# The up product's low parts of the two leading columns, multiplied in one run with the high columns

## Chip, cores and metric

The kernel runs on one core of a Trainium2 chip. The metric is device time in microseconds (us): the median of several runs, compared between the kernel before and the kernel after. TensorE multiplies matrices and adds into PSUM banks; VectorE (DVE) and ScalarE (ACT) do everything else on tiles in SBUF, GpSimd (POOL) does next to nothing here, and SyncE (SP) issues nearly all DMAs, in order.

## The reference

One layer of a decoder trunk, in float32, over 1024 tokens behind 16 meta tokens, with width 1024. Two mixers (a convolution branch and a sliding-window attention) are merged by gates; behind them stands a convolutional feed-forward part, which is where the change lies:

```python
    h = layer_norm(DEEPNORM_ALPHA * h + mixed @ w_out, ln1_g, ln1_b)
    up = causal_dwconv(h @ ffn_w_up, ffn_dw, ffn_dw_b)
    u, g = jnp.split(up, 2, axis=-1)
    f = (jax.nn.gelu(g, approximate=False) * u) @ ffn_w_down
    return layer_norm(DEEPNORM_ALPHA * h + f, ln2_g, ln2_b)
```

`ffn_w_up` is 1024 x 5632, `ffn_w_down` 2816 x 1024. The convolution has three taps over tokens and is causal, so each output token needs the up product of its own token and of the two before it.

## The kernel before

**Two-part numbers.** TensorE multiplies rounded float32 numbers. Each operand is split into a high part (ScalarE copies it into the rounded type) and a low part (VectorE subtracts the high part from the number). A product is then three matmuls: high weights with high tokens, high weights with low tokens, low weights with high tokens, all added into one bank.

**The up product.** `h @ ffn_w_up` is done in 22 chunks (`c`), each of 128 columns of u and the 128 columns of g that belong to them. A chunk is a Strassen-like product of two-by-two blocks, with seven products in place of eight. The token operand's seven blocks are B11, B21, BT2, BT1, BT3, BT4 and B22, sums and differences of quadrants (half of the model width, half of the tokens); the weights' seven are made chunk by chunk by `up_weights` (sums on L1426, splits in `wsplit`, L1408 and L1409). Each product has four steps of k (128 rows each), and each step the three matmuls above, on L1599.

**Token blocks.** The 512 tokens of each half are cut in two blocks, `SUB`, of 258 and 256 columns. The two columns more are the two leading columns that the convolution needs: block 0 starts two tokens early. B11, B21, BT2 and BT4 carry them (258 columns in block 0); BT1, BT3 and B22 don't (256), as `columns` says. For the second half the leading columns are those at the end of the first half, and L1652 copies them over.

**Banks.** Four PSUM tiles of 1024 columns hold the sums: pw (V4), px (X), pz (Z), py (Y). Block 0 lies in columns 254 to 511 of one bank and block 1 in 512 to 767 of the next. ScalarE copies X and Y out (L1611), VectorE forms the four results (L1607): c11 and c21 (with the leading columns), c12 and c22. `conv_ffn` applies the three taps: one ScalarE pass (L1523), two VectorE multiply-adds (L1524, L1525). After the gelu (L1529) and the product with the gate (L1533), the result is stored to DRAM (`fd`).

**Where the operands come from.** The low and high parts of the tokens are made once, by `bsplit` (L1279, L1284), from sums formed on L1288. Block 1's are ready first, so chunk 0 runs in two passes: block 1 alone, then block 0, for which the last rows of tokens are turned, summed and split while TensorE multiplies block 1. From chunk 1 on each product runs block 0 and block 1 one after the other (24 matmuls). The weights are split nine products ahead (`w_ahead`).

**Order.** On each engine the order of instructions is fixed when the program is built: a scheduler simulates the engines and takes, of the instructions that are ready, the one of lowest rank (`rank`; 400 for the evacuations of the up product, 470 for the tokens' sums, 500 for weight splits), with a few orders written by hand (`after`, `line`). So a new instruction may move others.

**Behind it.** The down product starts as soon as the last chunk's banks allow. Its operands are read back from `fd`, from `w_down`, or from sums of them (`sd`, `td`, formed on L1553 to L1563), cast on L1702, split on L1703 and multiplied on L1745. Its first product takes six pairs of operands; the sixth holds the last chunk's result.

The places of the tokens' blocks and the matmul loop:

```python
        return t[:, o + hl * 4 * n:o + (hl + 1) * 4 * n]
...
                        for j, (x, hl) in enumerate(((ah, 0), (ah, 1), (al, 0))):
                            ins = nc.tensor.matmul(o, x[:, ks], bmat(sub, q, hl, k), start=first and k + j == 0,
                                                   stop=k == 3 and j == 2, skip_group_check=not first)
```

Of the kernel before, what the change touches and what calls it, by code (L numbers as in the profile page):

```python
# [25 lines left out]
AF = mybir.ActivationFunctionType  # L26
# [75 lines left out]
def tile_hybrid_layer(  # L102
# [1136 lines left out]
    def columns(sub, q):  # L1239

        a, b = SUB[sub]
        return (2 if q in (BT1, BT3, B22) else a) if sub == 0 else a, b

    def bsum(sub, q, hl):
        a, b = columns(sub, q)
        n = b - a
        t, o = B_AT[sub][q]
        return t[:, o + hl * 4 * n:o + (hl + 1) * 4 * n]

    def bmat(sub, q, hl, k):  # L1250
        a, b = columns(sub, q)
        n = b - a
        return bsum(sub, q, hl)[:, k * n:(k + 1) * n]

    lined, high = [], []

# [9 lines left out]
    def wide(x):  # L1266
        return x.rearrange("p (k n) -> p k n", k=4)
# [4 lines left out]
    def bsplit(sub, q, src, cs=slice(None)):  # L1272
        with rank(RK_SUMS):
            a = columns(sub, q)[0] - SUB[sub][0]
            x, y, _ = cs.indices(SUB[sub][1] - SUB[sub][0])
            x = max(x, a)
            hi, lo = (wide(bsum(sub, q, hl))[:, :, x - a:y - a] for hl in range(2))
            src = wide(src)[:, :, x:y]
            ins = nc.scalar.copy(hi, src)  # L1279
            if (sub, q) in ((0, BT2), (0, BT4), (0, BT1), (0, BT3)):  # L1280
                if high:
                    after(ins, high[-1])
                high.append(ins)
            line(nc.vector.tensor_tensor(lo, src, f32(hi), OP.subtract))  # L1284

    def bsub(out, x, y, cs=slice(None)):
        with rank(RK_SUMS):
# [227 lines left out]
        ft_next[0] += 1  # L1515
        return FA[:, i * 512:(i + 1) * 512]

    c11, c21, u2 = (FA[:, 4128 + i * HW:4128 + (i + 1) * HW] for i in range(3))
    c12, c22, u13 = (RT[:, i * HW:(i + 1) * HW] for i in range(3))

    def conv_ffn(cc, o):
        t = ftmp()
        nc.scalar.activation(t, cc[:, 2:HW], AF.Identity, bias=ffw(3, o), scale=ffw(2, o))  # L1523
        nc.vector.scalar_tensor_tensor(t, cc[:, 1:HW - 1], ffw(1, o), t, OP.mult, OP.add)  # L1524
        nc.vector.scalar_tensor_tensor(t, cc[:, 0:HW - 2], ffw(0, o), t, OP.mult, OP.add)  # L1525
        return t

    def gelu(t):
# [40 lines left out]
    for c in range(FC):  # L1569
        if c == 1:  # L1570
            wo_stack.close()
            sums_p = ctx.enter_context(tc.tile_pool(name="sums", bufs=1, side="right", reuse_waits="tile"))
            RXF, SM1 = (sums_p.tile([P, 2048], F, name=n) for n in ("raw", "sums"))
            for i in range(FC):
                SM[i] = [(OB[:, 2048:4096], SM1)[i % 2][:, h * 1024:(h + 1) * 1024] for h in range(2)]
        V4, X, Z, Y = (pup.tile([P, 1024], F, name=n, tag=n) for n in ("pw", "px", "pz", "py"))
        passes = ((1,), (0,)) if c == 0 else ((0, 1),)
        for subs in passes:
            last = subs == passes[-1]
            w_next = iter(range(7))  # L1580
            a, b = SUB[subs[0]][0], SUB[subs[-1]][1]
            i = max(a, 2)

            def at(t, a=a):
                return t[:, 254 + a:254 + b]

            def prod(q, bank, first):
                if last:
                    w_ahead(9)
                    ah, al = w_ready.pop(0)  # L1590
                else:
                    ah, al = w_ready[next(w_next)]
                for sub in subs:
                    x, y = columns(sub, q)
                    o = bank[:, 254 + x:254 + y]
                    for k in range(4):
                        ks = slice(k * P, (k + 1) * P)
                        for j, (x, hl) in enumerate(((ah, 0), (ah, 1), (al, 0))):
                            ins = nc.tensor.matmul(o, x[:, ks], bmat(sub, q, hl, k), start=first and k + j == 0,  # L1599
                                                   stop=k == 3 and j == 2, skip_group_check=not first)  # L1600
                            if k + j == 0 and last_mm:
                                after(ins, last_mm[-1])
                    last_mm.append(ins)

            def tt(*x):
                with rank(RK_CHAIN):
                    return nc.vector.tensor_tensor(*x)  # L1607

            def copy(*x):
                with rank(RK_CHAIN):  # L1610
                    copied.append(nc.scalar.copy(*x))  # L1611
# [36 lines left out]
            if last:  # L1648
                with rank(RK_CHAIN):
                    ends, starts = (t.rearrange("p (i n) -> p i n", i=2)[:, :, x:x + 2]  # L1650
                                    for t, x in ((FA[:, 4128:4128 + 2 * HW], HW - 2), (RT[:, 0:2 * HW], 0)))
                    nc.vector.tensor_copy(starts, ends)  # L1652
# [278 lines left out]
```

## Time and profile before

| | |
|---|---|
| median of 3 runs | 1236.19 us (1235.96 to 1236.53) |
| span of the profiled execution, first to last instruction | 1234.6 us |
| TensorE's mean granted clock in it | 0.999 |
| up product (first to last start of a matmul of L1599) | 589.4 to 1017.3 us |
| of it chunk 0, in two passes | 589.4 to 611.2 us |
| down product | 1017.3 to the end |

The profile is of one execution; its own time is given as the span alone, and what lies around the span is the distance to the median. PE stands for TensorE's matmuls, PEld for its weight loads. A row of the timeline gives the start in us from the span's first instruction, the time from the start of the first to the end of the last instruction that it merges, then engine, line, operation, the tiles written and read, the shape, and the count; in brackets the idle time before it and what ended that. The ends of matmuls overlap with the next ones, so the pace of TensorE is read from the distance of starts.

### The profile page before, as it was taken

To read this page: it belongs to the slowest core of one execution; us is meant where nothing else is said; L and a number is where in the kernel's file an instruction comes from. 1 tells how busy PE (TensorE), PEld (TensorE's weight loads), DVE (VectorE), ACT (ScalarE), POOL (GpSimd) and SP (SyncE) were. 2 spreads that over 40 slices of the span, in tenths; PEclk is the share of its full clock that TensorE was granted. 3 is DMA by queue.
4 is the path that set the end of the run, shared out by engine and by line. 5 is a ranking of instruction groups with operands and counts; after the bars stand their busy time and mean duration, and the time that the engine had idled before them with its cause. 6 is when DMAs were issued, how large, how long until landed. Compare 5 with 4: busy or idle time off the path is not lost.

```text
span 1234.6 us, 21810 instructions
## 1 busy us (share of the span) xinstructions
PE 1225.2 (99%) x8568; PEld 1141.5 (92%) x8568; DVE 1085.2 (88%) x1842; ACT 584.7 (47%) x1065; POOL 15.6 (1%) x20
## 2 busy tenths in 40 slices
PE   9999999999999999999999999999999999999997
PEld 8999989999999999888999999999999998888886
DVE  8899989999879798659899999998999986996697
ACT  7532336654255223345755545555455554445331
POOL 1000000000000010000000000000000000000000
PEclk9999999999999999999999999999999999999999
DMA  7396834412255655322255555554455568988722
GB/s 282 74 298 151 210 98 116 127 55 73 82 158 163 183 140 144 104 85 87 66 171 207 191 187 205 188 183 142 172 203 190 178 239 304 391 315 312 256 86 85
DMA packets 109152, 213.02 MB, mean 173 GB/s; under 512 B 31883, under 2 KB 46779, under 8 KB 108922
## 3 DMA queue, kind: packets, MB, share of 16 engines
q1 hardware_dynamic: 93050, 200.56, 49.5%
q10 hardware_dynamic: 16000, 11.07, 2.9%
q8 instruction: 67, 1.10, 0.4%
q14 instruction: 35, 0.29, 0.1%
HBM read 149.98 MB, written 62.70 MB: 172 GB/s over the span
## 4 chain that ended last, share of the span: by engine, by line
PE 98%; DVE 1%; ACT 0%; issue 0%; DMA 0%; POOL 0%; DVEq 0%; POOLq 0%
PE px L1599 14%; PE py L1599 9%; PE ps_x L1745 9%; PE ps_z L315 8%; PE ps_z L314 8%; PE ps_z L310 8%; PE ps_z L1745 8%; PE pw L1599 5%; PE pz L1599 5%; PE ps_p L310 2%; PE ps_p L314 2%; PE ps_p L315 2%; PE ps_w L310 2%; PE ps_w L315 2%; PE ps_w L314 2%; PE ps_z L550 2%
## 5 line engine op out<-in xcount | busy, mean ns | idle before, releaser
L707 DVE SCALAR_TENSOR_TENSOR FA<-cin,cols,FA 128x1026 f32<-128x1026 f32 x120 | 152.2, 1277 | 0.9
L315 PE MATMUL ps_z<-RHO,wlo 128*128 128x256 f32 (+2 forms) x324 | 103.5, 320 | 0.0
L314 PE MATMUL ps_z<-RHO,whi 128*128 128x256 f32 (+2 forms) x324 | 103.4, 319 | 0.0
L315 PE MATMUL ps_z<-RHC,wlo 128*128 128x256 f32 (+2 forms) x324 | 103.4, 319 | 0.0
L314 PE MATMUL ps_z<-RHC,whi 128*128 128x256 f32 (+2 forms) x324 | 103.4, 319 | 0.0
L310 PE MATMUL ps_z<-RHO,whi 128*128 128x256 f32 (+2 forms) x324 | 103.3, 319 | 0.0
L310 PE MATMUL ps_z<-RHC,whi 128*128 128x256 f32 (+2 forms) x324 | 103.2, 319 | 0.0
L279 ACT CAST whi<-wr 128x1024 fp32r<-128x1024 f32 x37 | 38.9, 1050 | 107.4 <-PE ps_z L314 85.5
L1408 ACT CAST RHO<-wr 128x512 fp32r<-128x512 f32 x92 | 55.3, 619 | 25.3 <-DVE wr L1426 11.7
L1409 DVE TENSOR_TENSOR RHO<-wr,RHO 128x512 fp32r<-128x512 f32 x92 | 61.8, 684 | 5.1 <-ACT RHO L1408 5.0
L310 PEld LDWEIGHTS ps_z<-RHO,whi 128*128 128x128 f32 x324 | 60.9, 188 | 4.3
L314 PEld LDWEIGHTS ps_z<-RHO,whi 128*128 128x128 f32 x324 | 61.0, 188 | 4.2
L310 PEld LDWEIGHTS ps_z<-RHC,whi 128*128 128x128 f32 x324 | 60.9, 188 | 4.1
L314 PEld LDWEIGHTS ps_z<-RHC,whi 128*128 128x128 f32 x324 | 61.0, 188 | 4.0
L315 PEld LDWEIGHTS ps_z<-RHO,wlo 128*128 128x128 f32 x324 | 60.9, 188 | 4.0
L315 PEld LDWEIGHTS ps_z<-RHC,wlo 128*128 128x128 f32 x324 | 61.0, 188 | 3.9
L1426 DVE TENSOR_TENSOR wr<-wr 128x512 f32<-128x512 f32 x88 | 59.9, 681 | 0.2
L282 DVE TENSOR_TENSOR wlo<-wr,whi 128x1024 fp32r<-128x1024 f32 x35 | 42.7, 1220 | 11.8 <-ACT whi L279 11.4
L1611 ACT COPY FA<-px 128x514 f32<-128x514 f32 (+2 forms) x23 | 13.2, 572 | 70.7 <-PE px L1599 70.6
L1408 ACT CAST ws<-wr 128x512 fp32r<-128x512 f32 x60 | 36.1, 618 | 18.8 <-DVE wr L1426 10.7
L714 ACT ACTIVATE FA<-ps_z,cols 128x258 f32<-128x258 f32 (+2 forms) x48 | 26.1, 544 | 39.4 <-PE ps_z L315 36.6
L1599 PE MATMUL px<-OA,RHO 128*128 128x258 f32 (+1 forms) x336 | 43.8, 279 | 0.0
(491 smaller groups left out, 3488.2 us busy)
## 6 DMA issues: line engine op xcount, KB each, us to landing
wr<-in_w_up_dram SPq DMA_DIRECT2D x44, 512.0 KB, 4.6
wr<-in_w_z_dram SPq DMA_DIRECT2D x30, 512.0 KB, 3.9
fd<-FA SPq DMA_DIRECT2D x44, 256.0 KB, 2.4
OB<-in_w_down_dram SPq DMA_DIRECT2D x19, 512.0 KB
qt<-qd SPq DMA_DIRECT2D x28, 256.0 KB, 4.1
td<-OB SPq DMA_DIRECT2D x12, 512.0 KB
sums<-fd SPq DMA_DIRECT2D x12, 512.0 KB, 7.6
sd<-sums SPq DMA_DIRECT2D x12, 512.0 KB
```

What stands on the lines that cost most here:

```text
L279: ins = nc.scalar.copy(hi, raw)
L282: return (nc.vector if quick else nc.gpsimd).tensor_tensor(lo, raw, f32(hi), OP.subtract)
L310: ins = nc.tensor.matmul(ps, ah, bh, start=i == 0, stop=False)
L314: nc.tensor.matmul(ps, ah, bl, start=False, stop=False)
L315: last = nc.tensor.matmul(ps, al, bh, start=False, stop=i == n - 1)
L707: nc.vector.scalar_tensor_tensor(acc[c], cin[:, j:j + U], wc, acc[c], OP.mult, OP.add)
L714: nc.scalar.activation(t, ps, AF.Tanh, bias=bcol(14 + i), scale=0.5)
L1408: nc.scalar.copy(hi, src)
L1409: ins = nc.vector.tensor_tensor(lo, src, f32(hi), OP.subtract)
L1426: ins = nc.vector.tensor_tensor(*x)
L1599: ins = nc.tensor.matmul(o, x[:, ks], bmat(sub, q, hl, k), start=first and k + j == 0, stop=k == 3 and j == 2, skip_group_check=not first)
L1745: nc.tensor.matmul(bank[:, cs], l[:, ts], r[:, ws], start=first and a and x + k == 0, stop=z and x == len(ops) - 1 and k == 2, skip_group_ ...
```

## The change

In block 0 of B11, B21, BT2 and BT4 the high columns of a step of k (258) get the low parts of the two leading columns in front of them: 260 columns in a row. The three matmuls of a step are now high weights with these 260 columns, high weights with the remaining 256 low columns, and low weights with the 258 high columns. The first writes two columns more of the bank (252 and 253), which hold high weights times the low parts of the lead; VectorE adds them to the leading columns afterwards (`add_lead`, once for c11 and once for c21 in each chunk). The low block has 256 columns a step now, at a step of 256, and starts 1056 columns behind the high one. `bsplit` makes the low part of the lead in an instruction of its own. The results c11, c21, c12, c22 and the copies u2, u13 have rows of 516 columns in place of 514.

```diff
+    def leads(sub, q):
+        return sub == 0 and q in (B11, B21, BT2, BT4)
...
         t, o = B_AT[sub][q]
-        return t[:, o + hl * 4 * n:o + (hl + 1) * 4 * n]
...
+        n, step = ((260, 256)[hl], 1056) if leads(sub, q) else (256, 1024)
+        return t[:, o + hl * step:o + hl * step + 4 * n]
+
+    def runs(sub, q, k):
+        hi, lo = (wide(bsum(sub, q, hl))[:, k] for hl in range(2))
+        if leads(sub, q):
+            return (252, hi), (256, lo), (254, hi[:, 2:])
+        o = 256 + 256 * sub
+        return (o, hi), (o, lo), (o, hi)
...
-            hi, lo = (wide(bsum(sub, q, hl))[:, :, x - a:y - a] for hl in range(2))
-            src = wide(src)[:, :, x:y]
-            ins = nc.scalar.copy(hi, src)
+            hi, lo = (wide(bsum(sub, q, hl)) for hl in range(2))
+            src, x0 = wide(src), x
+            if leads(sub, q):
+                x0 = max(x, 2)
+                first, lo = hi[:, :, 0:2], lo[:, :, x0 - 2:y - 2]
+                hi = hi[:, :, 2:]
+            else:
+                lo = lo[:, :, x - a:y - a]
+            ins = nc.scalar.copy(hi[:, :, x - a:y - a], src[:, :, x:y])
...
-            line(nc.vector.tensor_tensor(lo, src, f32(hi), OP.subtract))
+            if x < x0:
+                line(nc.vector.tensor_tensor(first, src[:, :, 0:2], f32(hi[:, :, 0:2]), OP.subtract))
+            line(nc.vector.tensor_tensor(lo, src[:, :, x0:y], f32(hi[:, :, x0 - a:y - a]), OP.subtract))
...
+    HX = HW + 2
+    def add_lead(cc):
+        nc.vector.tensor_tensor(cc[:, 2:4], cc[:, 2:4], cc[:, 0:2], OP.add)
...
-                        for j, (x, hl) in enumerate(((ah, 0), (ah, 1), (al, 0))):
-                            ins = nc.tensor.matmul(o, x[:, ks], bmat(sub, q, hl, k), start=first and k + j == 0,
+                        for j, (x, (o, y)) in enumerate(zip((ah, ah, al), runs(sub, q, k))):
+                            ins = nc.tensor.matmul(bank[:, o:o + y.shape[-1]], x[:, ks], y, start=first and k + j == 0,
...
             if last:
+                with rank(RK_CHAIN):
+                    add_lead(c11)
                 g0 = gelu(conv_ffn(c11, FC + c))
...
             if last:
                 with rank(RK_CHAIN):
+                    add_lead(c21)
```

More of the change, by code (lines that the diff above doesn't have):

```diff
@@ L1516, in ftmp @@
         return FA[:, i * 512:(i + 1) * 512]
-    c11, c21, u2 = (FA[:, 4128 + i * HW:4128 + (i + 1) * HW] for i in range(3))
-    c12, c22, u13 = (RT[:, i * HW:(i + 1) * HW] for i in range(3))
+    HX = HW + 2
+    c11, c21, u2 = (FA[:, 4128 + i * HX:4128 + (i + 1) * HX] for i in range(3))
+    c12, c22, u13 = (RT[:, i * HX:(i + 1) * HX] for i in range(3))
+    def add_lead(cc):
+        nc.vector.tensor_tensor(cc[:, 2:4], cc[:, 2:4], cc[:, 0:2], OP.add)
     def conv_ffn(cc, o):
         t = ftmp()
-        nc.scalar.activation(t, cc[:, 2:HW], AF.Identity, bias=ffw(3, o), scale=ffw(2, o))
-        nc.vector.scalar_tensor_tensor(t, cc[:, 1:HW - 1], ffw(1, o), t, OP.mult, OP.add)
-        nc.vector.scalar_tensor_tensor(t, cc[:, 0:HW - 2], ffw(0, o), t, OP.mult, OP.add)
+        nc.scalar.activation(t, cc[:, 4:HX], AF.Identity, bias=ffw(3, o), scale=ffw(2, o))
+        nc.vector.scalar_tensor_tensor(t, cc[:, 3:HX - 1], ffw(1, o), t, OP.mult, OP.add)
+        nc.vector.scalar_tensor_tensor(t, cc[:, 2:HX - 2], ffw(0, o), t, OP.mult, OP.add)
         return t
@@ L1580, in tile_hybrid_layer @@
             w_next = iter(range(7))
[L1581 to L1582 removed]
+            a, b = SUB[subs[0]][0] + (2 if subs[0] else 0), SUB[subs[-1]][1] + 2
+            i = max(a, 4)
             def at(t, a=a):
[L1585 removed]
+                return t[:, 252 + a:252 + b]
             def prod(q, bank, first):
```

10 lines of the change are left out of this document (1 added, 9 removed).

## The prediction

> **What bounds the kernel now.** I read the page's busy table and chain of waits first. The second row below is the chain, by engine.
>
> ```profile
> PE 1225.2 (99%) x8568; PEld 1141.5 (92%) x8568; DVE 1085.2 (88%) x1842; ACT 584.7 (47%) x1065; POOL 15.6 (1%) x20
> PE 98%; DVE 1%; ACT 0%; issue 0%; DMA 0%; POOL 0%; DVEq 0%; POOLq 0%
> ```
>
> TensorE is busy 99% of the span and is 98% of the chain, so a change is worth what it takes from TensorE's own time, less any wait that it puts in TensorE's way. The up product's matmuls all stand on L1599. The view of that line lists how long TensorE sat idle ahead of them:
>
> ```profile
>   DVE OA L1284: 1.0, 2
>   ACT OB L1611: 0.3, 1
> ```
>
> 1.3 us in three waits is all, over the whole up product; none is for weights (L1409) and none for a bank that VectorE empties. The busy table of one long window, 640 to 1000 us (PE, PEld, DVE, ACT, POOL, then the granted clock, the DMA share and GB/s), shows the steady state:
>
> ```profile
> 640.00:1000.00 360.00, 360.00 (x3131) 360.00 (x3131) 336.55 (x555) 191.25 (x318) 0.00 (x0) 1.00 0.54 189
> ```
>
> TensorE is full at full clock, VectorE 93% full. So two things are to be priced: how fast the matmuls follow each other, and whether VectorE, which gets more to do, ever becomes late.
>
> For the first I use the start times in TensorE's timeline. "Busy" per matmul (276 to 283 ns) contains overlap; the distance between the starts of two groups of 12 does not.
>
> ```profile
> 707.95 1.59 PE L1599 MATMUL px<-RHC,RHO 128*128 128x258 f32 x12
> 709.38 1.52 PE L1599 MATMUL px<-OC,RHO 128*128 128x256 f32 x12
> 710.74 1.60 PE L1599 MATMUL pz<-RHO 128*128 128x258 f32 x12
> 712.18 1.52 PE L1599 MATMUL pz<-OC,RHO 128*128 128x256 f32 x12
> 713.54 1.59 PE L1599 MATMUL px<-OA,RHO 128*128 128x258 f32 x12
> ```
>
> Twelve matmuls of 256 columns take 1.36 us, 113.3 ns each and 0.443 ns a column. Twelve of 258 take 1.43 or 1.44 us, 119.5 ns each. Two columns at 0.443 ns would be 0.9 ns; the difference is 6.2. A 258-column matmul thus pays some 5.3 ns more than its columns. The rows also show that the cheap rate comes back with the very next group: 256 after 258 costs 1.36 us every time.
>
> **The change, part by part.** Each of B11, B21, BT2, BT4 in token block 0 has four steps of k, and each step three matmuls: high weights with high tokens, high with low, low with high. Before, all three are 258 wide. Now they are 260, 256 and 258 wide, because the low parts of the two leading columns are multiplied in the first. On TensorE, before and now, the first of these products in chunk 0 (px is bank X, W the weights):
>
> ```order
> L1599 MATMUL px<-RHC,W_5846 128x258 x12
> L1599 MATMUL pz<-RHO,W_5846 128x258 x12
> L1599 MATMUL px<-OA,RHO 128x258 x12
> L1599 MATMUL pw<-OA,RHO 128x258 x12
> L1599 MATMUL py<-RX,RHO 128x256 x12
> ```
>
> ```order
> L1618 MATMUL pw<-OA,RHO 128x260
> L1618 MATMUL pw<-OA,RHO 128x256
> L1618 MATMUL pw<-OA,RHO 128x258
> L1618 MATMUL pw<-OA,RHO 128x260
> L1618 MATMUL pw<-OA,RHO 128x256
> L1618 MATMUL pw<-OA,RHO 128x258
> ```
>
> The second piece is half of the product into pw. The number of matmuls and of weight loads is the same, and the columns too: 260 + 256 + 258 = 3 x 258 = 774. The number of triples is 4 products x 4 k x 22 chunks = 352.
>
> *The middle matmul.* 258 to 256 columns: from 119.5 to 113.3 ns if it runs like its neighbours of 256, 6.2 x 352 = 2.2 us less. The trace has no single 256 between two other widths, so I bound it. Not every 256-column matmul gets 113.3 ns:
>
> ```profile
> 589.36 1.58 PE L1599 MATMUL px<-OC,W 128*128 128x256 f32 x12
> 590.77 1.58 PE L1599 MATMUL pz<-OC,W 128*128 128x256 f32 x12
> 1225.42 1.60 PE L1745 MATMUL ps_z<-RHC,RHO 128*128 128x256 f32 x12
> 1226.86 0.52 PE L1745 MATMUL ps_z<-RHO 128*128 128x256 f32 x3
> ```
>
> In chunk 0 twelve take 1.41 us (117.5 each), in the last products 1.44 us (120 each). So 256 columns have a fast and a slow pace; at the slow one the gain is 0. Between 0 and 2.2 us I take 2.2, because in the steady state the fast pace returns right behind every 258 group.
>
> *The first matmul.* 260 columns are not in the trace. Two columns more at 0.443 ns are 0.9 ns, 0.3 us over 352. If 260 had the fast pace (260 x 0.443 = 115.2 ns) it would gain 4.3 ns instead, 1.5 us. I take the loss of 0.3, as the nearest width, 258, never shows the fast pace.
>
> *The third matmul* keeps 258 columns and starts two columns further into its block: 0, bounded by the fast pace for 258 (114.2 ns), a gain of 5.3 x 352 = 1.9 us.
>
> *VectorE and ScalarE in the steady state.* Each chunk gets two adds of 128x2 (the lead's sum) and two columns more on the evacuations. The nearest row for a tiny operation is the copy of L1652:
>
> ```profile
> 978.58 0.17 DVE L1652 COPY OB<-FA 128x4 f32<-128x4 f32 x1
> 978.70 0.69 DVE L1561 TENSOR_TENSOR sums<-sums 128x512 f32<-128x512 f32 x1
> ```
>
> The next operation starts 0.12 us later, so two adds cost 0.24 us of a chunk's 19.3. VectorE idles more than that in every chunk, waiting for a bank's copy that TensorE paces (columns: us in all, times, longest):
>
> ```profile
> DVE OB L1607 <- ACT OB L1611: 12.9, 19, 1.5
> ```
>
> 12.9 us in 19 waits is 0.7 us a chunk. That is the cover, and I cost the adds at 0; with no cover they would be 0.24 x 22 = 5.3 us.
>
> *Chunk 0.* Here VectorE is late already. It forms the low parts of the tokens just ahead of TensorE:
>
> ```profile
> 601.51 0.42 DVE L1607 TENSOR_TENSOR OB<-OB 128x256 f32<-128x256 f32 x1
> 601.84 0.41 DVE L1607 TENSOR_TENSOR FA<-OB,pw 128x256 f32<-128x256 f32 x1
> 602.17 1.22 DVE L1284 TENSOR_TENSOR OA<-OB,OA 128x1032 fp32r<-128x1032 f32 x1
> 603.34 1.69 PE L1599 MATMUL px<-OA,RHO 128*128 128x258 f32 x12
> 603.65 0.68 DVE L1426 TENSOR_TENSOR wr<-wr 128x512 f32<-128x512 f32 x1
> 604.25 1.22 DVE L1284 TENSOR_TENSOR OA<-FA,OA 128x1032 fp32r<-128x1032 f32 x1
> 604.87 0.28 PE L1599 MATMUL pw<-OA,RHO 128*128 128x258 f32 x1
> 605.39 0.42 DVE L1607 TENSOR_TENSOR FA<-pz,OB 128x258 f32<-128x258 f32 x1
> 605.53 1.57 PE L1599 MATMUL pw<-OA,RHO 128*128 128x258 f32 x11 [0.38 <-DVE OA L1284]
> 605.73 1.22 DVE L1284 TENSOR_TENSOR RX<-FA,RX 128x1024 fp32r<-128x1024 f32 x1
> 606.86 2.35 DVE L1284 TENSOR_TENSOR OA<-FA,OA 128x1024 fp32r<-128x1024 f32 x2
> 606.94 1.63 PE L1599 MATMUL py<-RX,RHO 128*128 128x256 f32 x12
> 608.40 1.58 PE L1599 MATMUL px<-OA,RHO 128*128 128x256 f32 x12
> ```
>
> The second matmul of BT4 (into pw) waits for BT4's low part: it starts 0.66 us after the first instead of 0.12, a loss of 0.54. VectorE's order there before, and then now (now L1299 the lead's low part, L1300 the rest, L1626 evacuations, L1442 weight sums):
>
> ```order
> L1607 TENSOR_TENSOR OB<-OB 128x256
> L1607 TENSOR_TENSOR FA<-OB,pw 128x256
> L1284 TENSOR_TENSOR OA<-OB,OA 128x1032
> L1607 TENSOR_TENSOR OB<-py,FA 128x256
> L1426 TENSOR_TENSOR wr<-wr 128x512
> L1284 TENSOR_TENSOR OA<-FA,OA 128x1032
> L1607 TENSOR_TENSOR FA<-pz,OB 128x258
> L1284 TENSOR_TENSOR RX<-FA,RX 128x1024
> ```
>
> ```order
> L1626 TENSOR_TENSOR OB<-OB 128x256
> L1626 TENSOR_TENSOR FA<-OB,pw 128x256
> L1626 TENSOR_TENSOR OB<-py,FA 128x256
> L1299 TENSOR_TENSOR OA<-OB,OA 128x4x2
> L1300 TENSOR_TENSOR OA<-OB,OA 128x1024
> L1299 TENSOR_TENSOR OA<-FA,OA 128x4x2
> L1300 TENSOR_TENSOR OA<-FA,OA 128x1024
> L1442 TENSOR_TENSOR wr<-wr 128x512
> L1674 COPY OB<-FA 128x2x2
> L1626 TENSOR_TENSOR FA<-pz,OB 128x260
> L1300 TENSOR_TENSOR RX<-FA,RX 128x1024
> ```
>
> An evacuation (0.33 us) and the lead (0.12) now come ahead of BT2's low part, while the weight sum (0.6) and an evacuation (0.34) come behind BT4's, ahead of BT1's (RX). Counting starts from 601.51 with these steps: BT2's low part begins at 602.62 and is done at 603.8, where TensorE wants it at 603.46, a wait of 0.35. TensorE then ends BT2 at 605.16 and finds BT4's low part ready (605.05): the 0.54 is gone. BT1's begins at 606.07 and is done at 607.26, TensorE wants it at 606.71: a new wait of 0.55. BT1 so ends at 608.56, against 608.40 in the rows. The waits change places and the sum is a loss of 0.2 us.
>
> *The hand-over to the down product.* There the cover is thin. The chain starts with the last store of the up product (the first two rows, from chunk 20, show the step of a multiply-add):
>
> ```profile
> 1008.95 0.75 DVE L1525 SCALAR_TENSOR_TENSOR FA<-OB,cols,FA 128x512 f32<-128x512 f32 x1
> 1009.62 0.75 DVE L1524 SCALAR_TENSOR_TENSOR FA<-FA,cols 128x512 f32<-128x512 f32 x1
> ...
> 1035.29 0.68 DVE L1533 TENSOR_TENSOR FA<-FA 128x512 f32<-128x512 f32 x1
> 1038.05 0.32 SPq L113 DMA_DIRECT2D FA<-fd  x1
> 1043.25 0.62 ACT L1702 CAST RHO<-OB 128x512 fp32r<-128x512 f32 x1 [1.47 <-DMA OB<-td]
> 1043.90 0.69 DVE L1703 TENSOR_TENSOR RHO<-OB,RHO 128x512 fp32r<-128x512 f32 x1 [1.40 <-ACT RHO L1702]
> 1044.50 2.93 PE L1745 MATMUL ps_z<-RHO,RHC 128*128 128x512 f32 x12
> ```
>
> The product L1533 is stored, read back behind it in SP's queue, cast and split, and VectorE ends at 1044.59, when TensorE has already begun with the high part. About 0.1 us of slack. If TensorE comes 1.7 us earlier and this chain doesn't, the gain is lost there. The chain's earlier end is chunk 20's second product, on VectorE before and now:
>
> ```order
> L1607 TENSOR_TENSOR FA<-pz,OB 128x514
> L1533 TENSOR_TENSOR FA<-FA 128x512
> L1525 SCALAR_TENSOR_TENSOR FA<-OB,cols,FA 128x512
> L1524 SCALAR_TENSOR_TENSOR FA<-FA,cols 128x512
> L1525 SCALAR_TENSOR_TENSOR FA<-FA,cols 128x512
> L1533 TENSOR_TENSOR FA<-FA 128x512
> ```
>
> ```order
> L1546 SCALAR_TENSOR_TENSOR FA<-OB,cols,FA 128x512
> L1725 TENSOR_TENSOR OC<-wr,OC 128x1024
> L1626 TENSOR_TENSOR FA<-pz,OB 128x516
> L1554 TENSOR_TENSOR FA<-FA 128x512 x2
> ```
>
> Two multiply-adds fewer stand ahead of that store, and everything behind it in SP's queue (the sums' loads, then the operands' loads) can start that much earlier. So I expect the chain to move with TensorE, or more, at no cost.
>
> *The sum.* -2.2 + 0.3 + 0.2 = -1.7 us. The profiled execution's span is 1234.6 us, so 1232.9 after; the median of the runs, 1236.19, lies 1.6 us above that span for what is around it. That gives 1234.5 us, 0.14% less.
>
> **The rivals.** *More: the first and third matmul take the fast pace too* once the middle one breaks the row of 258s. All three at 0.443 ns a column are 774 x 0.443 = 342.9 ns against 358.5; 15.6 x 352 = 5.5 us less, with chunk 0 a time of 1230.9. For it: the pace of a 256 group changes from one stretch to the next, so it is a state and no fixed price. Against it: none of the 258 groups ever has it. Part of it (one of the two) is 1232 to 1233.5.
>
> *Columns alone count.* The triple has 774 columns before and after; if the 6.2 ns belong to the triple and not to the one matmul, nothing is gained and chunk 0's loss stays: 1236.4. Against it stands the quick return to 1.36 us in the rows. The Trainium skill says as much in TensorE: Matmul & The Clock Gate, section Back-to-back issue gap: a warm matmul follows the last after N / 2.4 ns + 2.5 ns. By it 258 and 256 differ by an estimated 0.8 ns and this change is worth nothing on TensorE; the measured 6.2 ns disagrees with the rule for these two widths, so I give the rival little.
>
> *Slower: the last store comes late.* The order behind it in chunk 21 changes too, and its operands' splits can slip ahead of the last product. By their starts a split of 1024 columns takes 1.14 us (606.86 less 605.73 for the like form) and a multiply-add 0.66; two splits and one multiply-add are 2.9 us. TensorE, 1.7 us early with 0.1 of slack, would wait 4.5 us: -1.7 + 4.5 = +2.8, 1239.0. It decides from a slip of 2.6 us on; a smaller one only eats the gain. For it: the slack of 0.1 us. Against it: the earlier store of chunk 20.
>
> **How the numbers follow.** What a measurement of this kernel can tell from no change is about 0.2%, 2.5 us: faster means under 1233.7. Forecast 0.46, of which a quarter (0.12) falls under 1233.7, as one more matmul in a few gets the fast pace; more, 0.30; columns alone 0.10; slower 0.14. Faster is 0.12 + 0.30 = 0.42, same 0.34 + 0.10 = 0.44, slower 0.14. The forecast's own range, from the slow pace in half of the middle matmuls (1.1 us) to the fast pace in a part of the first ones, is 1233.4 to 1235.8. The range to hold 8 in 10 reaches half way to the other cases on both sides: 1231.6 to 1237.0.
>
> **What would show it.** In the new timeline, a product of mixed widths taking 1.41 to 1.42 us for twelve (one matmul in three cheaper by 6.2, one dearer by 0.9, so 1.434 - 0.021) shows the matmul step right; 1.43 shows the columns rule, 1.37 the larger gain. In chunk 0, waits ahead of BT2's and BT1's second matmul instead of BT4's show that step right. TensorE idle at the down product's sixth operand pair, or a split between the last multiply-add and the last product, would show the hand-over wrong. Idle time of L1618 for weights would show that VectorE's cover was smaller than 0.24 us a chunk.

## The result and the profile after

The changed kernel takes 1240.05 us (median of 5 runs, 1239.97 to 1240.32) against 1236.19 us before (5 runs, 1235.96 to 1236.53): the ratio is 1.0032 [1.0020, 1.0044]. It is 3.9 us slower, and the forecast was 1.7 us faster. The profiled execution's span is 1238.2 us, 3.6 us more than before.

The page of the changed kernel, busy table and chain of waits, gives no hint: TensorE is as full as it was.

```profile
PE 1228.9 (99%) x8568; PEld 1145.2 (92%) x8568; DVE 1088.3 (88%) x1890; ACT 585.1 (47%) x1065; POOL 15.6 (1%) x20
PE 98%; DVE 1%; ACT 0%; issue 0%; DMA 0%; POOL 0%; DVEq 0%; POOLq 0%
```

The number of matmuls is the same, 8568, and TensorE is busy 3.7 us longer. Most of that isn't waiting; the same work runs slower. The idle time ahead of the up product's instructions (now L1618) in the changed kernel (us in all, times) shows how little is waiting:

```profile
its engine sat idle before it (us, times) until:
  DVE OA L1300: 1.6, 2
  DVE RX L1300: 0.6, 2
```

2.2 us against 1.3, all of it in chunk 0. This view counts a wait twice, for the matmul and for the weight load ahead of it; the matmuls alone stood idle for 0.88 us against 0.48 before. There is still no wait for weights or for a bank.

The pace has to be read from the distance of starts, for one whole chunk. First the length of a chunk before, in TensorE's timeline: the first product (B11, block 0) of two chunks in a row.

```profile
649.95 1.59 PE L1599 MATMUL px<-RHC,RHO 128*128 128x258 f32 x12
...
669.28 1.60 PE L1599 MATMUL px<-RHC,ws 128*128 128x258 f32 x12
```

19.33 us. The same chunk in the changed kernel (a row of 260 is a product of mixed widths: the row names the width of its first matmul):

```profile
650.30 1.61 PE L1618 MATMUL px<-RHC,RHO 128*128 128x260 f32 x12
651.75 1.57 PE L1618 MATMUL px<-OC,RHO 128*128 128x256 f32 x12
653.16 1.59 PE L1618 MATMUL pz<-RHO 128*128 128x260 f32 x12
654.59 1.55 PE L1618 MATMUL pz<-OC,RHO 128*128 128x256 f32 x12
655.98 1.61 PE L1618 MATMUL px<-OA,RHO 128*128 128x260 f32 x12
657.42 1.57 PE L1618 MATMUL px<-OC,RHO 128*128 128x256 f32 x12
658.83 1.59 PE L1618 MATMUL pw<-OA,RHO 128*128 128x260 f32 x12
660.26 1.55 PE L1618 MATMUL pw<-RHC,RHO 128*128 128x256 f32 x12
661.65 1.52 PE L1618 MATMUL py<-RX,RHO 128*128 128x256 f32 x12
663.01 1.52 PE L1618 MATMUL py<-OC,RHO 128*128 128x256 f32 x12
...
669.81 1.61 PE L1618 MATMUL px<-RHC,ws 128*128 128x260 f32 x12
```

19.51 us. The four mixed products take 1.45, 1.43, 1.44 and 1.43 us, hardly more than the 1.43 and 1.44 of the 258s before. The loss stands in the rows *between* them, which the change doesn't touch: twelve matmuls of 256 columns take 1.41, 1.39, 1.41 and 1.39 us there, where each took 1.36 before. From 661.65 on, where no product is mixed, it is 1.36 again.

With the starts in full, as means over chunks 1 to 21: mixed products 1.445 and 1.432 us in turn (before 1.434), the groups behind them 1.412 and 1.385 (before 1.360). That is 84 mixed products x 4.2 ns = 0.35 us, and 42 x 52 + 42 x 25 ns = 3.2 us in the groups behind; chunk 0 adds 0.24 (22.11 us against 21.87, from its first matmul to that of chunk 1). The sum is 3.8 us, and the up product takes 431.75 us (589.18 to 1020.93) against 427.93.

Inside the groups, the distances of single starts in the trace (ns, means over chunks 1 to 20; for the kernel before, 2 to 20) show that this is a pace, not a single stumble:

```
behind B11, BT2:  117 118 117 118 117 118 118 118 117 118 118 117
behind B21, BT4:  123 122 117 116 114 113 113 113 113 113 113 113
before, all four: 113 113 113 113 113 113 113 113 113 113 113 113
```

A matmul of 256 columns has a fast pace of 113.3 ns and a slow one of 117.7. Behind B11 and BT2 the slow one runs to the end of the group; behind B21 and BT4 it gives way after four matmuls. From chunk to chunk the time of a group repeats to 1 ns, while the DMA moves between 143 and 207 GB/s in the same stretch (619 to 990 us, by the slices of the page) and the split weights go round ten places in memory, seven a chunk. So a collision with the DMA's traffic, or the place of the weights, is an unlikely cause.

The rest of the changed kernel did what was expected. Chunk 0, its timeline, TensorE's rows and VectorE's low parts (L1299, L1300):

```profile
602.57 1.22 DVE L1300 TENSOR_TENSOR OA<-OB,OA 128x1024 fp32r<-128x1024 f32 x1
...
602.84 0.31 PE L1618 MATMUL px<-OA,RHO 128*128 128x260 f32 x1
...
603.84 1.58 PE L1618 MATMUL px<-OA,RHO 128*128 128x256 f32 x11 [0.69 <-DVE OA L1300]
...
605.25 1.62 PE L1618 MATMUL pw<-OA,RHO 128*128 128x260 f32 x12
...
605.93 1.21 DVE L1300 TENSOR_TENSOR RX<-FA,RX 128x1024 fp32r<-128x1024 f32 x1
...
606.71 0.29 PE L1618 MATMUL py<-RX,RHO 128*128 128x256 f32 x1
...
607.19 1.54 PE L1618 MATMUL py<-RX,RHO 128*128 128x256 f32 x11 [0.20 <-DVE RX L1300]
...
608.57 1.18 PE L1618 MATMUL px<-OA,RHO 128*128 128x256 f32 x9
```

BT4's product (pw, 605.25) now runs through in one piece; BT2 and BT1 wait ahead of their second matmul instead. In the long window, 640 to 1000 us, VectorE is 94% full, with 33 more instructions (588 in place of 555):

```profile
640.00:1000.00 360.00, 360.00 (x3104) 360.00 (x3103) 337.58 (x588) 190.77 (x316) 0.00 (x0) 1.00 0.53 186
```

TensorE is full at a granted clock of 1.00 there, and yet gets 3104 matmuls done, not 3131: 27 fewer. And the last group of the down product, TensorE's timeline:

```profile
1230.46 0.52 PE L1767 MATMUL ps_z<-RHO 128*128 128x256 f32 x3
```

It starts 209.53 us behind the end of the up product (1020.93); before, 1226.86 less 1017.28 is 209.58. Nothing was lost behind the up product.

### The profile page after: what moved, and what is told of

Its sections match the earlier page's. It is cut to its first block, busy times and chain, and to the rows that moved or that the text cites. A ratio compares the mean times of both kernels' runs of the same rounds, so it can differ in the third digit from the quotient of the medians.

```text
span 1238.2 us, 21853 instructions
## 1 busy us (share of the span) xinstructions
PE 1228.9 (99%) x8568; PEld 1145.2 (92%) x8568; DVE 1088.3 (88%) x1890; ACT 585.1 (47%) x1065; POOL 15.6 (1%) x20
## 4 chain that ended last, share of the span: by engine, by line
PE 98%; DVE 1%; ACT 0%; issue 0%; DMA 0%; POOL 0%; DVEq 0%; POOLq 0%
PE px L1618 15%; PE py L1618 9%; PE ps_x L1767 9%; PE ps_z L315 8%; PE ps_z L314 8%; PE ps_z L310 8%; PE ps_z L1767 8%; PE pz L1618 5%; PE pw L1618 5%; PE ps_p L310 2%; PE ps_p L314 2%; PE ps_p L315 2%; PE ps_w L310 2%; PE ps_w L315 2%; PE ps_w L314 2%; PE ps_z L550 2%
## 5 line engine op out<-in xcount | busy, mean ns | idle before, releaser
L1630 ACT COPY FA<-px 128x516 f32<-128x516 f32 (+2 forms) x23 | 13.2, 573 | 72.1 <-PE px L1618 72.1
L1618 PE MATMUL px<-OA,RHO 128*128 128x260 f32 (+1 forms) x336 | 44.1, 280 | 0.7 <-DVE OA L1300 0.7
```

The source lines that it names most:

```text
L1618: ins = nc.tensor.matmul(bank[:, o:o + y.shape[-1]], x[:, ks], y, start=first and k + j == 0, stop=k == 3 and j == 2, skip_group_check=not ...
```

## The experiments

Three things could have slowed TensorE's untouched groups: VectorE's new work and the new layout in memory, the mixed widths and the order in which they follow each other, or the places of the columns. All kernels below are the changed kernel or the one before with one edit. Times are medians of ten runs (four for the 272-column steps, one for the added matmul), group times are means over chunks 1 to 21, by starts; "mixed" are the four products of the leads, "behind" the four groups of 256 that follow them, "others" the six that are left.

**Widths on the old layout.** The kernel before, with its layout and its VectorE work; only TensorE's runs get the new widths. The 260 columns so begin 8 bytes earlier and the 256 begin 8 bytes later than the 258 did, and the low parts of the lead are left out.

```diff
-                        for j, (x, hl) in enumerate(((ah, 0), (ah, 1), (al, 0))):
-                            ins = nc.tensor.matmul(o, x[:, ks], bmat(sub, q, hl, k), ...
+                        hi, lo = (bmat(sub, q, hl, k) for hl in range(2))
+                        runs = (o, hi), (o, lo), (o, hi)
+                        if y - x == 258:
+                            t, c = B_AT[sub][q]
+                            runs = ((bank[:, 252:512], t[:, c + k * 258 - 2:c + k * 258 + 258]),
+                                    (bank[:, 256:512], lo[:, 2:]), (o, hi))
+                        for j, (w, (o_, r)) in enumerate(zip((ah, ah, al), runs)):
+                            ins = nc.tensor.matmul(o_, w[:, ks], r, ...
```

> The kernel before, with nothing changed but the three widths in the mixed products (260, 256, 258; the two columns more are read from what lies in front of the block, and the low parts of the two leading columns are left out). Inherited pace: the groups of 256 behind a mixed product run slow (1.38 to 1.41 us for twelve in place of 1.36) though VectorE, the layout and the order are those of before; 1238 to 1240.5 us. VectorE or layout at fault: groups of 256 stay at 1.36, 1234 to 1236.5 us.

Measured: 1238.37 us (1238.23 to 1239.29), ratio 1.0018 [1.0008, 1.0027]. Its TensorE timeline:

```profile
649.82 1.62 PE L1605 MATMUL px<-RHC,RHO 128*128 128x260 f32 x12
651.28 1.52 PE L1605 MATMUL px<-OC,RHO 128*128 128x256 f32 x12
652.64 1.62 PE L1605 MATMUL pz<-RHO 128*128 128x260 f32 x12
```

The mixed product takes 1.46 us, 27 ns *more* than twelve matmuls of 258, and the group behind it 1.36. So the new widths, with their shifted starts, cost 2.2 us with VectorE and the layout as they were. The time is within the range for an inherited pace, but its mechanism isn't seen here: the cost lies in the mixed product and not behind it.

**The order of the matmuls.** The changed kernel with everything but the order of the twelve matmuls kept: in the first the low columns (256) come last in each step, in the second behind all four steps' high runs, (260, 258) four times and then 256 four times.

```diff
-                    for k in range(4):
+                    steps = [(k, j) for k in range(4) for j in range(3)]
+                    if leads(sub, q):
+                        steps = [(k, j) for k in range(4) for j in (0, 2, 1)]
+                    for i, (k, j) in enumerate(steps):
...
```

> The changed kernel with the three matmuls of a step in another order: high weights with high (260), low weights with high (258), high weights with low (256), so that a mixed product ends on a 256. Inherited pace: the next group of 256 starts in the fast pace and takes 1.36 us; a mixed product takes about 1.42 to 1.43 us; 1235 to 1236.5 us. VectorE or layout at fault: no change, 1240 us. The width of 260 at fault by itself: mixed products stay at 1.43 to 1.445, about 1236.5 us, with groups of 256 at 1.36.

```diff
+                    if leads(sub, q):
+                        steps = [(k, j) for k in range(4) for j in (0, 2)] + [(k, 1) for k in range(4)]
```

> The changed kernel with the four 256 matmuls of a mixed product put together at its end: 260, 258 four times, then 256 four times. Inherited pace: the four run at 113 to 114 ns, the product takes about 8 x 120 + 4 x 113.5 = 1.414 us, and the group of 256 behind it 1.36; 1234 to 1235.5 us. VectorE or layout at fault: 1240 us.

Measured: 1237.07 us (1236.91 to 1237.34), 1.0007 [0.9998, 1.0017], and 1235.95 us (1235.85 to 1236.16), 0.9997 [0.9987, 1.0006]. TensorE's timeline of the second:

```profile
652.49 1.59 PE L1621 MATMUL pz<-RHO 128*128 128x260 f32 x12
653.92 1.52 PE L1621 MATMUL pz<-OC,RHO 128*128 128x256 f32 x12
655.28 1.59 PE L1621 MATMUL px<-OA,RHO 128*128 128x260 f32 x12
656.70 1.52 PE L1621 MATMUL px<-OC,RHO 128*128 128x256 f32 x12
```

The group behind a mixed product is at 1.36 again (1.363 in the first kernel, 1.360 in the second), with the same weights, columns, places, VectorE instructions and widths as in the changed kernel. In the first, VectorE's and ScalarE's instructions even stand in the same order; only the order within the twelve matmuls differs. So neither VectorE nor the layout by itself costs anything there: the order of the matmuls does, through what it leaves behind. (Width, weights and place change their order together, so these two runs can't tell which of them counts.) Both times lie above what an inherited pace had been given, as the mixed products, at 1.437 and 1.427 us, are slower than the 1.42 and 1.414 expected. The second's mixed product takes 1.427 us, 7 ns less than the 258s; that is the whole gain on TensorE, 84 x 7 ns = 0.6 us, too little to stand clear of the kernel before.

**The middle matmul by itself.** This is the prediction's term of -2.2 us, alone: the kernel before with the middle run of each step cut to 256 columns (they begin 8 bytes later).

```diff
+                        if y - x == 258:
+                            runs = (o, hi), (bank[:, 256:512], lo[:, 2:]), (o, hi)
```

> The kernel before with the middle matmul of each step alone made 256 wide (258, 256, 258; the high weights' product with the low parts of the two leading columns is left out). It measures the term of 6.2 ns a middle matmul by itself. As the prediction had it: mixed products 1.434 - 0.025 = 1.409 us, groups behind them 1.36, 1234.0 us. If a 256 between two 258s takes no fast pace: 1.43 us or more, 1236 us or more, with groups behind at 1.36 to 1.41.

Measured: 1238.90 us; eight runs at 1238.8 to 1238.9, two at 1245.7 and 1245.8 (the ratio of means, 1.0034 [1.0019, 1.0049], holds these two). The profiled execution is one of the eight:

```profile
649.85 1.58 PE L1603 MATMUL px<-RHC,RHO 128*128 128x258 f32 x12
651.26 1.58 PE L1603 MATMUL px<-OC,RHO 128*128 128x256 f32 x12
652.68 1.61 PE L1603 MATMUL pz<-RHO 128*128 128x258 f32 x12
654.12 1.54 PE L1603 MATMUL pz<-OC,RHO 128*128 128x256 f32 x12
655.50 1.58 PE L1603 MATMUL px<-OA,RHO 128*128 128x258 f32 x12
...
669.32 1.58 PE L1603 MATMUL px<-RHC,ws 128*128 128x258 f32 x12
```

The mixed products take 1.415 and 1.444 us in turn: the first is what the prediction named as the sign of a right matmul step (1.41 to 1.42), the second is not. The groups behind take 1.413 and 1.381; these and the time fit the expectation for a 256 that takes no fast pace. The chunk is 19.47 us, 0.13 more than before. So 32 columns fewer a chunk (16 middle matmuls, two each) make the kernel 2.7 us slower, and no new instruction on any engine has a part in it.

**The places of the columns.** The changed kernel with steps of 272 columns and blocks moved so that high and low blocks start on multiples of 128 bytes (counted from their tile's start; 272 columns are 1088 bytes, so the steps of a high block start 0 and 64 bytes behind a multiple in turn), and the kernel before with nothing but BT3's block 0 moved by 64 bytes, from 64 behind a multiple of 128 onto a multiple. No widths are mixed in the second.

```diff
-    B_AT = [[(RHC, 6224), (RHO, 4112), (OA, 16), (RX, 48), (OA, 2096), (OA, 6224), (OA, 4144)],
+    B_AT = [[(RHC, 6208), (RHO, 4096), (OA, 0), (RX, 48), (OA, 2112), (OA, 6208), (OA, 4160)],
...
-        n, step = ((260, 256)[hl], 1056) if leads(sub, q) else (256, 1024)
+        n, step = ((272, 256)[hl], 1088) if leads(sub, q) else (256, 1024)
```

> The changed kernel with the steps of a high block 272 columns apart in place of 260, so that every 260 starts at the same place within 64 bytes. If the start address of the columns within such a line sets the pace, the period of the mixed product changes (all four steps alike) and with it the pace of the group behind it, to anything from 1.36 to 1.41 us; 1235.5 to 1240 us. If address plays no part, groups stay at 1.445, 1.41, 1.43, 1.385: 1240 us.

```diff
-    B_AT = [[(RHC, 6224), (RHO, 4112), (OA, 16), (RX, 48), (OA, 2096), (OA, 6224), (OA, 4144)],
+    B_AT = [[(RHC, 6224), (RHO, 4112), (OA, 16), (RX, 48), (OA, 2080), (OA, 6224), (OA, 4144)],
```

> The kernel before with one block of tokens (BT3, block 0, 256 columns) moved down by 64 bytes, from a place 64 bytes behind a multiple of 128 to a multiple of 128. Address sets the pace: the group of BT3's block 0 takes 1.41 to 1.42 us in place of 1.36 in every chunk, perhaps the group behind it 1.36 to 1.39; up to 22 x 0.06 = 1.3 us, or 2 us with the next group: 1237 to 1238.3 us. Address plays no part: 1.36 and 1236.2 us.

Measured: 1241.70 us (1241.48 to 1241.92), 1.0045 [1.0030, 1.0060], and 1238.42 us (1238.08 to 1239.56), 1.0019 [1.0009, 1.0028]. TensorE's timeline of the second, from the group ahead of BT3's block 0 on:

```profile
662.43 1.52 PE L1599 MATMUL py<-OC,RHO 128*128 128x256 f32 x12
663.79 1.59 PE L1599 MATMUL px<-OA,ws 128*128 128x256 f32 x12
665.21 1.55 PE L1599 MATMUL px<-RHC,ws 128*128 128x256 f32 x12
666.60 1.52 PE L1599 MATMUL py<-OA,ws 128*128 128x256 f32 x12
667.96 1.52 PE L1599 MATMUL py<-RHC,ws 128*128 128x256 f32 x12
```

The moved group takes 1.42 us (1.428 in the mean) where it took 1.36, the next, unmoved, 1.39, and the one behind that 1.36. VectorE's and ScalarE's instructions stand in the same order as before. So the place of the columns that a matmul reads changes the pace too, and again the next group inherits it. The first kernel shows both: its mixed products take 1.421 us, less than the 1.445 and 1.432 of the changed kernel, but the blocks of BT3 and B22 that had to move by the same 64 bytes take 1.421 in place of 1.360, and the groups behind them 1.379. Both times came out above the ranges given for an address that counts (by 1.7 and 0.1 us).

**Inherited or set by the place?** In the changed kernel the leads' blocks all start 64 bytes behind a multiple of 128, in equal steps, and yet B11 and BT2 differ from B21 and BT4. If the pace is inherited, a group's pace depends on the group ahead. Two kernels ask for that. The first lets the mixed product end with 258 and 256 columns, not 256 and 258; the second puts one matmul of 64 columns between the mixed product and the next group (it begins a sum of its own in a bank that is still adding, so that product's sums are changed).

```diff
+                    if leads(sub, q):
+                        steps = steps[:10] + [(3, 2), (3, 1)]
```

> The changed kernel with one pair of matmuls swapped, the last two of a mixed product: ...260, 258 (low weights), 256 (high with low). Inherited pace, from the last matmul: groups behind a mixed product take 1.36 to 1.37 us in place of 1.41 and 1.385, the mixed product stays at 1.43 to 1.445; 1236 to 1237.5 us. If the pace is set by the whole mixture, groups stay at 1.385 to 1.41: 1239.5 to 1240 us.

```diff
+                    if leads(sub, q):
+                        gap = nc.tensor.matmul(bank[:, 0:64], al[:, 384:512], hi_0[:, 0:64], start=True, stop=True)
```

> The changed kernel with one matmul of 64 columns (into columns of the bank that nothing uses) between a mixed product and the group of 256 behind it. Inherited pace: the groups behind no longer take 1.412 and 1.385 in turn; another end leaves another pace, 1.36 or 1.41 for all of them. The added matmul itself costs some 0.04 to 0.1 us x 84, 3 to 8 us, so 1240 to 1248 us in all; the groups' times in the trace decide. Pace set by the place of the columns alone: 1.412 and 1.385 as before.

The first: seven runs at 1239.3 to 1239.6 us and three at 1247.8 to 1247.9; the ratio of means is 1.0046 [1.0025, 1.0067]. The profiled execution (span 1245.8 us) is one of the three, and its TensorE timeline shows what they are:

```profile
659.55 1.60 PE L1621 MATMUL pw<-OA,RHO 128*128 128x260 f32 x12
660.98 1.58 PE L1621 MATMUL pw<-RHC,RHO 128*128 128x256 f32 x12
662.40 1.58 PE L1621 MATMUL py<-RX,RHO 128*128 128x256 f32 x12
663.81 1.58 PE L1621 MATMUL py<-OC,RHO 128*128 128x256 f32 x12
665.22 1.58 PE L1621 MATMUL px<-OA,ws 128*128 128x256 f32 x12
```

Every group of 256 takes 1.41 us, all through the up product, also the six that don't follow a mixed product. The slow pace is kept up at the very places that run at 1.36 in the changed kernel. The program is the same in all ten runs, so it doesn't settle the pace alone. The seven shorter runs weren't profiled; that they have the fast pace in the groups of 256 further behind is argued from their time: six groups in 21 chunks at 53 ns each are 6.7 of the 8.3 us. Their median lies where a pace set by the whole mixture was expected (1239.5); two times for one kernel were not expected.

The second (one run, 1248.56 us), its TensorE timeline:

```profile
655.35 0.19 PE L1624 MATMUL pz<-RHO 128*128 128x64 f32 x1
655.38 1.63 PE L1619 MATMUL pz<-OC,RHO 128*128 128x256 f32 x12
656.85 1.61 PE L1619 MATMUL px<-OA,RHO 128*128 128x260 f32 x12
658.29 0.19 PE L1624 MATMUL px<-OA,RHO 128*128 128x64 f32 x1
658.32 1.63 PE L1619 MATMUL px<-OC,RHO 128*128 128x256 f32 x12
659.78 1.61 PE L1619 MATMUL pw<-OA,RHO 128*128 128x260 f32 x12
```

The alternation is gone. Behind the short matmul each group starts with one distance of 196 ns, then 118 to 120, and is at 113 from the sixth on: 1.465 us for every one, where 1.36 or 1.41 was expected. And now every mixed product takes 1.445 us, what only B11 and BT2 took in the changed kernel, and its twelve distances are those of B11 there to 1 ns. That fits one reading of the rows after: a mixed product that follows a group ending in the fast pace (B11, BT2) takes 1.445 and leaves the slow pace; one that follows a group in the slow pace (B21, BT4) takes 1.432 and leaves a pace that decays. By this reading products alternate because each inherits what the other left.

**Can a rule be had?** Three more kernels tried to predict the pace. All of 260, then all of 258, then all of 256:

```diff
+                        steps = [(k, j) for j in (0, 2, 1) for k in range(4)]
```

> The changed kernel with a mixed product's matmuls ordered by width: four of 260, four of 258, four of 256. If only the run of four 256 at the end counts, as in the kernel with the lows put last, 1.427 us a product and 1.36 behind it, 1235.9 us. If the change of width from one matmul to the next costs too, 1.41 to 1.42 and 1234.5 to 1235.5 us.

The order (260, 258) four times, then 256 four times, with B11's high block put 112 bytes behind a multiple of 128, in steps of 288 columns:

```diff
+    def block(sub, q, hl):
+        if (sub, q, hl) == (0, B11, 0):
+            return wide(RHC[:, 7232:8384])[:, :, 28:288]
+        if (sub, q, hl) == (0, B11, 1):
+            return wide(RHC[:, 6224:7248])
+        return wide(bsum(sub, q, hl))
```

> The kernel with the lows put last, and the high block of one product, B11, laid so that all four 260 runs start 112 bytes behind a multiple of 128 (the place of the fourth step, where 260 and 258 took 115 and 116 ns there). Address sets the pace: B11's mixed product takes 4 x 115 + 4 x 116 + 470 = 1.39 us in place of 1.427, 22 x 0.035 = 0.8 us in all, 1235.2 us. Address plays no part: 1.427 and 1235.9 us.

And the same order with steps of 264 columns, no block moved:

```diff
-        n, step = ((260, 256)[hl], 1056) if leads(sub, q) else (256, 1024)
+        n, step = ((264, 256)[hl], 1056) if leads(sub, q) else (256, 1024)
```

> The kernel with the lows put last, with the high block's steps 264 columns apart in place of 260 (places 64, 96, 0 and 32 bytes behind a multiple of 128). A search for a better layout, with no forecast of its own from either theory beyond this: if places matter, mixed products leave 1.427 us for something between 1.39 and 1.45, and the groups behind either stay at 1.36 or go to 1.41; 1234 to 1239 us.

Measured: 1237.92 us (nine runs at 1237.6 to 1238.3, one at 1244.7), ratio 1.0019 [1.0008, 1.0030], with the groups behind at 1.413 and 1.360 in turn, though the product ends in four matmuls of 256; 1239.05 us (1238.73 to 1239.35), 1.0023 [1.0013, 1.0032], with B11 itself at 1.448 and the groups behind B11 and B21 at 1.413; and 1236.01 us (1235.80 to 1236.36), 0.9998 [0.9989, 1.0008], with nothing changed by the steps. The first two came out otherwise than either theory had it. The second of them has the clearest case of a pace handed on: B21 and BT2 aren't moved in it, stand where the kernel with the 256s behind all has them, and yet take 1.435 and 1.436 us in place of 1.427. No rule that I tried gives the pace from widths and places. What stands is that the order of the matmuls counts, that the places count, and that the pace is carried on; no kernel changes a width and leaves the places as they are.

All of them together (us; two numbers stand for products in turn; the groups of the swapped kernel are those of its one trace, of a run at 1247.8; the kernel before ran along with each set, at 1236.19 to 1236.25):

| kernel | median | mixed | behind | others | chunk |
|---|---|---|---|---|---|
| before | 1236.19 | 1.434 | 1.360 | 1.360 | 19.34 |
| after | 1240.05 | 1.445, 1.432 | 1.412, 1.385 | 1.360 | 19.51 |
| new widths, on before | 1238.37 | 1.461 | 1.359 | 1.360 | 19.44 |
| 256 last in a step | 1237.07 | 1.437 | 1.363 | 1.360 | 19.36 |
| 256s behind all | 1235.95 | 1.427 | 1.360 | 1.360 | 19.31 |
| middle alone, on before | 1238.90 | 1.415, 1.444 | 1.413, 1.381 | 1.360 | 19.47 |
| steps of 272 | 1241.70 | 1.421 | 1.393 | 1.421, 1.379 in BT3 and B22 | 19.57 |
| BT3 moved by 64 bytes, on before | 1238.42 | 1.434 | 1.360 | 1.428, 1.385 in BT3 | 19.43 |
| last two swapped | 1239.49 | 1.433 | 1.413 | 1.413 | 19.87 |
| short matmul between | 1248.56 | 1.445 | 1.465 | 1.360 | 19.92 |
| by width | 1237.92 | 1.426, 1.421 | 1.413, 1.360 | 1.360 | 19.40 |
| B11 at 112 bytes | 1239.05 | 1.448 (B11), 1.427 to 1.436 | 1.413 (B11, B21), 1.360 | 1.360 | 19.45 |
| 256s behind, steps of 264 | 1236.01 | 1.427 | 1.360 | 1.360 | 19.31 |

No version is clearly below the kernel before: the two that lie below it, those with the 256s behind all, have intervals that hold 1.

## Why the prediction was wrong

*The middle matmul, -2.2 us.* This is the step that failed: "Between 0 and 2.2 us I take 2.2, because in the steady state the fast pace returns right behind every 258 group." It read the 1.36 us behind a row of twelve 258s as what any 256 does behind a wider one. The reading under it, "256 after 258 costs 1.36 us every time", doesn't hold for the kernel before either. In chunk 1 the group of 256 behind B11's twelve 258s takes 1.41 us (TensorE's timeline before), with the slow pace in all twelve distances:

```profile
612.66 1.58 PE L1599 MATMUL px<-OC,ws 128*128 128x256 f32 x12
614.07 1.60 PE L1599 MATMUL pz<-RHO,ws 128*128 128x258 f32 x12
```

The last groups of chunk 0 ran at 1.41 us too, so the pace was already handed on there, through a product of 258s. Measured by itself, the cut gives 4 ns a product (1.434 to the mean of 1.415 and 1.444), 0.4 us in all, and takes 3.1 us back in the groups behind (42 x 53 + 42 x 21 ns). The bounds were at fault as well: 0 to 2.2 us left no room for a loss. The prediction had a row that should have opened them, chunk 0's 256 columns at 1.41 us, and even called the pace "a state and no fixed price" under a rival; it didn't follow that a state can be left behind in groups that the diff doesn't touch. Those groups were priced at nothing without being named.

*The first matmul, +0.3, and the third, 0.* Not separable in the changed kernel. From the middle cut alone (mean 1.430) to the changed kernel (mean 1.438) a mixed product takes 9 ns more, 0.8 us over 84 where 0.3 was said, but in another layout, so this isn't the size of the two terms.

*VectorE, 0.* Right as far as the runs show. The kernel with the 256s behind all has the adds, the leads' own low parts and the wider evacuations, and loses nothing (1235.95 us).

*Chunk 0, +0.2.* Right in the waits, in part lucky in the size (+0.24). The waits stand where they were said to: BT4's is gone, BT2's low part is done at 603.79 (603.8 was said), BT4 starts at 605.25 (605.16), BT1's first matmul at 606.71 (606.71), the product behind it at 608.57 (608.56). BT2's wait was longer than said, since TensorE came at 602.84 and not 603.34, but its end was set by VectorE. Up to the product behind BT1 chunk 0 had lost 0.35 us, counted from the up product's first matmul (589.18, before 589.36). Two groups there then ran at 1.36 us, where they took 1.42 and 1.41 before, and gave 0.11 back; the prediction had no such term.

*The hand-over, 0.* Right as far as seen: no idle time at the down product, 209.5 us as before. The changed kernel came late and didn't try the slack of 0.1 us; the one with the 256s behind all ended its up product at 1016.53, 0.75 us earlier than before, and its down product took no longer.

*The rivals.* "Slower" came true in sign alone (1239.0 was its time): its place, the last store, had no part. "More" was wrong: no mixed product came near 1.37 us, though single ones of 260 and 258 did reach the fast pace (115 and 116 ns in the fourth step of the kernel with the 256s behind all; 115.2 and 114.2 would be that pace). "Columns alone" comes nearest for the mixed product itself, 1.438 in the mean against 1.434. The formula of the Trainium skill that stood beside it (TensorE: Matmul & The Clock Gate, section Back-to-back issue gap) is meant there for isolated matmuls, and the section says that in a stream of weight loads and matmuls, as here, both set the spacing. A formula in the width alone gives a width one gap; the rows give 256 columns two, 113.3 and 117.7 ns at the same granted clock, and the measurement decides.

*Slips in the sums.* The 1.3 us of idle time "in three waits" counts weight loads with the matmuls, which alone waited twice, 0.48 us. The forecast's own upper bound comes out at 1235.6 by its own terms (1234.5 + 1.1), not 1235.8, and half way from 1234.5 to the cases at 1230.9 and 1239.0 is 1232.7 and 1236.8, not 1231.6 and 1237.0. None of this changes the account: 1240.05 lies outside either way.

*What stays open.* Where the pace is kept, and what in the order of the matmuls and the places of columns picks it. That it is kept is shown by the order experiments (same groups, other neighbours), the short matmul (alternation gone), the moved B11 (unmoved products change) and the swapped one (1.41 us throughout); how it comes about is not. One trail stands in the traces: the weight loads differ with the pace. In the six groups behind no mixed product, over chunks 1 to 21, a weight load of the kernel before starts 110 ns ahead of its matmul and takes 187 or 188 ns, every one of 1512. In the trace of the swapped kernel, where all of them run at 117.8 ns, it starts 114 or 115 ns ahead, and a third of them (504) take 192 ns. So loads and matmuls fall into step in two ways; whether that makes the pace or follows from it, no run here shows.

## What to carry to other kernels

On a kernel whose TensorE is full, compare the distance of starts of the neighbours of a changed group, not of the group alone: here the touched products moved by 4 ns in the mean and the untouched ones behind them by 25 to 52. Before a layout is rebuilt for a few columns, run the new widths by themselves on the old layout; one run of the middle matmul by itself would have shown that the term to be gained wasn't there. And when a run of columns is changed or moved, try the order of the matmuls around it too, since that alone was worth 4.1 us here.

## What was not expected of the hardware

Matmuls of one shape (256 columns), at one granted clock and with nothing to wait for, follow each other at 113.3 or at 117.7 ns, and the pace is handed on: it can hold for a whole up product (every group of 256 columns 1.413 us in an execution of 1245.8 us span, while seven other runs of that kernel took 8.3 us less), or give way after four or five matmuls. A shift of one block by 64 bytes, with nothing else changed, took its twelve matmuls from 1.360 to 1.428 us and the kernel from 1236.25 to 1238.42.
